# One decoder layer on one core: row numbers copied one by one for the gathered rows, and the first up loads placed behind the down loads on SyncE

## The chip, the core and the metric

The kernel runs on one core of a Trainium2 chip. The metric is device time in microseconds (us) of one execution; lower is better. Engines are named as the profile names them: PE is TensorE, DVE is VectorE, ACT is ScalarE, POOL is GpSimd, SP is SyncE, which here only issues DMAs.

## The reference, cut to what matters

One decoder layer: a mixing part (mLSTM and windowed attention), a cross-attention part, and the PEER part, in which this change lies.

```python
# per block of 128 tokens, xb: (128, 1024); 8 heads, top 16 of 128*128 experts each
qh = (xb @ w_pq)...; s1, s2 = scores against two key sets (128 keys each)
eidx, g = top 16 of the summed scores per head, softmax over them
u = expert_down[eidx]                            # rows of a 16384 x 1024 table
a = gelu(einsum('thkd,td->thk', u, xb))
out = einsum('thk,thkd->td', g * a, expert_up[eidx])
```

## The kernel before, in words

The 512 tokens are four blocks of 128. Block 0 follows the reference word for word: for each of its 128 choices per token a **fetch** (an indirect DMA on POOL, L767) brings one table row per token into one of eight buffers named `rows` (0.5 MB each), and DVE multiplies it with the tokens (L773, result in a column of `dots`); after 128 such products come 128 fetches from the up table, added up by DVE (L783, `gacc`). These 256 steps are a Python generator, `gather`; the body calls `step(ga, 1)` wherever one is to be placed.

Blocks 1 to 3 are computed densely. A **down tile** (`Down`) holds 128 experts: SP loads two tiles at a time into `draw` (L825, 1 MB, two buffers), ACT and DVE split each into a high and a low part (`dh` L790, `dl` L828), PE runs 24 matmuls (L839 to L841) into `acc_d`, and ACT applies gelu. An **up tile** (`up_tile`) needs the gates of its experts (`wt`, L873, three loads per four tiles, one for each block), the up table (`uraw`, L881, two tiles per load), and runs its matmuls at L912 to L914. There are 128 of each. Down tiles 0 to 71 are computed early, as filler beside other stages; their results go to DRAM (L863).

The gates come from two places. Those of block 1 are scattered to DRAM by POOL (L690). Those of blocks 2 and 3 are computed by `gating`: 32 steps `q` per block, in each of which DVE writes four one-hot tiles (`oh`, L744; the one for a whole step at L721 or by ACT at L725), PE multiplies them (L745, tile `w`), ACT copies the result to `stg` (L747, two buffers), and PE fills the rest of the step with nine matmuls of a down tile. Every eighth step the 2 MB in `stg` are stored to DRAM by a DMA that ACT issues (L749, `wd<-stg`).

In block 3, at the twelve odd steps from 9 to 31 (`GQ`), one step of the gather is made. After the gating come seven **lead** tiles (down tiles 72 to 78, `LEAD`), with ten gather steps among them (`GLD`), so 22 products in all before the up tiles start. The fetches of these 22 read the row numbers directly from `c.eidx`; after the lead, DVE copies the whole of `c.eidx` into `rowid` (L1209), and all later fetches read that copy and so cannot be issued before it.

The framework orders the instructions of each engine by a simulated schedule. `tc.issue_after(i)` adds an order edge for the instructions made in the block that run on the engine of `i`, and no wait. Each engine runs its list in order; so does SP with its DMA issues: one that waits for a semaphore holds all behind it.

Of the kernel before, what the change touches and what calls it, by code (L numbers as in the profile page):

```python
# [14 lines left out]
I32 = mybir.dt.int32  # L15
U32 = mybir.dt.uint32
AF = mybir.ActivationFunctionType
ALU = mybir.AluOpType
# [3 lines left out]
P = 128  # L22
# [3 lines left out]
NB = S // P  # L26
# [14 lines left out]
UG = 4  # L41
# [9 lines left out]
GQ = range(9, 32, 2)  # L51
GLD = 10
GST = 120
WST, WTL = 3, 5


LEAD = 7
# [15 lines left out]
GRP = 2  # L73
# [625 lines left out]
def gating(c, early, ga):  # L699

    nc, ps, gs, mp = c.nc, c.ps, c.gs, c.mp
    V, A, T = nc.vector, nc.scalar, nc.tensor
    for b in range(NG + NS, NB):
        tr = []
        for n_, src in (("I1T", c.I1), ("I2T", c.I2), ("gT", c.gg)):
            tp = ps.tile([P, 512], F32, tag="a", name="tp_i")
            tr_ = T.transpose(tp[:, :P], src[:, b].rearrange("p h k -> p (h k)"), c.ident)
            o = gs.tile([P, P], F32, tag=n_, bufs=1, name=n_)
            A.copy(o, tp[:, :P])
            tr.append(o)  # L710
        i1, i2, g = tr
        n1 = gs.tile([P, P], F32, tag="n1", bufs=1, name="n1")
        A.mul(n1, i1, -1.0)
        io = c.iota.unsqueeze(1).to_broadcast([P, 4, P])

        def onehot(q):

            o1 = gs.tile([P, 4, P], F32, tag="oh1", bufs=5, name="oh1")
            ib = i1[:, 4 * q:4 * q + 4].unsqueeze(2).to_broadcast([P, 4, P])
            if q % 2:  # L720
                V.tensor_tensor(o1, io, ib, op=ALU.is_equal)  # L721
            else:
                for t1 in range(4):
                    t = 4 * q + t1
                    A.activation(o1[:, t1], c.iota, AF.Abs, bias=n1[:, t:t + 1])  # L725
                A.activation(o1, o1, AF.Relu, bias=1.0, scale=-1.0)
            return o1

        oh = [onehot(q) for q in range(3)]
        if b == NG + NS:  # L730
            with c.tc.issue_after(tr_.ins):
                early.fill(FGT0)
        for q in range(32):
            if q % 8 == 0:
                stg = gs.tile([P, NK, 32], F32, tag="stg", bufs=2, name="stg")
            if q + 3 < 32:
                oh.append(onehot(q + 3))
            o1 = oh[q]
            w = ps.tile([P, 512], F32, tag="b", name="w")
            w4 = w.rearrange("p (i t) -> p i t", t=4)  # L740
            for t1 in range(4):
                t = 4 * q + t1
                o2 = gs.tile([P, P], F32, tag="oh2", bufs=4, name="oh2")
                last = V.tensor_scalar(o2, c.iota, i2[:, t:t + 1], g[:, t:t + 1], op0=ALU.is_equal, op1=ALU.mult)  # L744
                mm = T.matmul(w4[:, :, t1], o1[:, t1], o2, start=True, stop=True)  # L745
            q8 = q % 8
            A.copy(stg[:, :, 4 * q8:4 * q8 + 4], w4)  # L747
            if q8 == 7:
                nc.scalar.dma_start(c.wd[b - NG][:, :, 32 * UG * (q // 8):32 * UG * (q // 8 + 1)].rearrange("g p i -> p g i"),  # L749
                                  stg.rearrange("p (g i) t -> p g (i t)", i=UG))  # L750
            with c.tc.issue_after(mm.ins):
                early.fill(FGT)
            if b == NB - 1 and q in GQ:
                with c.tc.issue_after(c.sc[HD - 1][-1].ins), c.tc.issue_after(last.ins):
                    step(ga, 1)


def gather(c):

    nc, gp, mp = c.nc, c.gp, c.mp  # L760
    V, A, G = nc.vector, nc.scalar, nc.gpsimd
    dots = gp.tile([P, P], F32, name="dots")
    c.gacc = gp.tile([P, D], F32, name="gacc")

    def fetch(src, j):
        r = gp.tile([P, D], F32, tag="rows", bufs=8, name="rows")
        G.indirect_dma_start(out=r, out_offset=None, in_=src,  # L767
                             in_offset=bass.IndirectOffsetOnAxis(ap=c.rowid[:, j:j + 1], axis=0))
        return r

    for j in range(P):
        r = fetch(c.a["down_r"], j)
        V.tensor_tensor_reduce(r, r, c.xn0, 1.0, 0.0, op0=ALU.mult, op1=ALU.add, accum_out=dots[:, j:j + 1])  # L773
        yield
    coef = gp.tile([P, P], F32, name="coef")
    A.activation(coef, dots, AF.Gelu)
    V.tensor_tensor(coef, coef, c.gg[:, 0].rearrange("p h k -> p (h k)"), op=ALU.mult)
    for j in range(P):
        r = fetch(c.a["up"], j)
        if j == 0:  # L780
            V.tensor_scalar(c.gacc, r, coef[:, j:j + 1], None, op0=ALU.mult)
        else:
            V.scalar_tensor_tensor(c.gacc, r, coef[:, j:j + 1], c.gacc, op0=ALU.mult, op1=ALU.add)  # L783
        yield


def split3(c, pool, raw, tag, bufs):
# [29 lines left out]
class Down:  # L817


    def __init__(self, c, i2):  # L820
        nc, dp = c.nc, c.dp
        self.c, self.i2 = c, i2
        if i2 % GRP == 0:
            c.draw = dp.tile([P, GRP, D], F32, tag="draw", bufs=2, name="draw")
            nc.sync.dma_start(c.draw, c.a["down_t"][i2 // GRP])  # L825
        raw = c.draw[:, i2 % GRP]
        self.hi, self.lo = split3(c, dp, raw, "d", 2)
        c.dl = nc.vector.tensor_tensor(self.lo, raw, f32(self.hi), op=ALU.subtract)  # L828
        self.acc = None
        self.k = 0  # L830
# [36 lines left out]
def up_tile(c, u, i2, gel, acc):  # L867
    nc, up = c.nc, c.up
    V, A, T = nc.vector, nc.scalar, nc.tensor
    if i2 % UG == 0:  # L870
        c.wt = up.tile([P, ND, UG * P], F32, tag="wt", bufs=2, name="wt")
        for b in range(ND):
            i = nc.sync.dma_start(c.wt[:, b], c.wd[b][i2 // UG])  # L873
            for j in c.sc[HD - 1] if b == 0 else ():
                c.tc.add_manual_dep(i.ins, j.ins.name, SYNC, reason="gates complete")
        if i2 < SP:
            c.gsr = c.gl.tile([P, UG, TD], F32, tag="gsr", bufs=2, name="gsr")
            nc.sync.dma_start(c.gsr, c.gd[i2 // UG])
    if i2 % GRP == 0:
        c.uraw = up.tile([P, GRP, D], F32, tag="uraw", bufs=3, name="uraw")  # L880
        nc.sync.dma_start(c.uraw, c.a["up"].rearrange("(i p) d -> p i d", p=P)[:, i2:i2 + GRP])  # L881
    g = c.gsr[:, i2 % UG] if i2 < SP else gel[i2]
    raw = c.uraw[:, i2 % GRP]
    last = u == NK - 1
    if last:
        z = c.xlo.rearrange("p k t -> p (k t)")
        hi, lo = z[:, 0:D], z[:, D:2 * D]
        A.copy(hi, raw)
    else:
        hi, lo = split3(c, up, raw, "u", 2)  # L890
    V.tensor_tensor(lo, raw, f32(hi), op=ALU.subtract)  # L891
    cf = up.tile([P, TD], F32, tag="cf", bufs=2, name="cf")
    if last:
        ch, cl = z[:, 2 * D:2 * D + TD], z[:, 3 * D:3 * D + TD]
    else:
        ch = up.tile([P, TD], F32R, tag="ch", bufs=2, name="ch")
        cl = up.tile([P, TD], F32R, tag="cl", bufs=2, name="cl")
    c.cf = V.tensor_tensor(cf.rearrange("p (b t) -> p b t", t=32), g.rearrange("p (b t) -> p b t", t=32),
                    c.wt.rearrange("p b (q i t) -> p (b q) i t", q=4, i=UG)[:, :, i2 % UG], op=ALU.mult)
    A.copy(ch, cf)  # L900
    c.cl = V.tensor_tensor(cl, cf, f32(ch), op=ALU.subtract)  # L901
    return hi, lo, ch, cl
# [230 lines left out]
def body(tc, a, out, dbg=None):  # L1133
    c = Ctx()
    c.tc, c.nc, c.a = tc, tc.nc, a
    nc = c.nc
    with ExitStack() as st:
# [55 lines left out]
            ws.close()  # L1193
        c.gl = st.enter_context(pool("gels"))
        with pool("gather", side="right") as c.gp:
            c.rowid = c.eidx
            ga = gather(c)
            with pool("gating") as c.gs:
                gating(c, early, ga)
            c.up = st.enter_context(pool("up"))  # L1200
            assert len(gel) == SP

            for n in range(LEAD):
                ahead(1)
                with tc.issue_after(c.dl.ins):
                    step(ga, GLD * (n + 1) // LEAD - GLD * n // LEAD)
            c.rowid = c.gp.tile([P, P], I32, name="rowid")
            with tc.issue_after(c.dl.ins):
                nc.vector.tensor_copy(c.rowid, c.eidx)  # L1209
            pst_ = [c.ps.tile([P, 512], F32, tag=t, name="acc_u") for t in "bbbbaa"]  # L1210
            acc = [[pst_[2 * b], pst_[2 * b + 1]] for b in range(ND)]
            last, mms = [], []
            g0 = len(GQ) + GLD
            due = [WST * u + WTL * made_by(u) for u in range(-1, GST)]
            rows = [(2 * P - g0) * (d - due[0]) // (due[-1] - due[0]) for d in due]
            rows += [rows[-1]] * (NK - GST)
            for u, i2 in enumerate(up_order()):
# [49 lines left out]
def step(it, n):  # L1267
    for _ in range(n):
        next(it, None)
# [49 lines left out]
```

## Time and profile before

| | us |
|---|---|
| median of 3 runs | 1648.53 (1648.18 to 1648.61) |
| the profiled execution, its own time | 1650.35 |
| its span in the trace | 1648.70 |
| mean granted clock of TensorE | 0.991 |
| PE busy | 1605.7 (97%) |
| DVE busy | 1233.7 (75%) |
| ACT busy | 723.2 (44%) |
| POOL busy | 590.8 (36%) |

The span runs from the first to the last instruction in the trace. A stretch of the trace is named by its us from the start of the span. The last gating block runs from 781 to 866 us, the lead from there to 892, the up tiles from there to the end.

### The profile page before, as it was taken

What the parts mean: (1) busy time and instruction counts of PE and PEld (TensorE: products, weight loads), DVE (VectorE), ACT (ScalarE), POOL (GpSimd) and SP (SyncE); (2) the same over time, 40 slices, a digit from 0 to 9 for tenths busy, and PEclk for the clock granted to TensorE, in tenths of its full rate; (3) what the DMA queues carried; (4) which work ended last, traced back from release to release, by engine and by line L of the source; (5) the groups of instructions that cost most, each with busy time, mean ns of one, the idle gap of its engine ahead of it and who ended that gap; (6) DMA issues with size and microseconds to landing.
All of it is one profiled execution on the core that took longest, in us unless ns stands there. A gap on an engine that the chain in (4) does not pass through costs nothing.

```text
span 1648.7 us, 23081 instructions
## 1 busy us (share of the span) xinstructions
PE 1605.7 (97%) x8387; PEld 1411.7 (86%) x8388; DVE 1233.7 (75%) x2704; ACT 723.2 (44%) x1217; POOL 590.8 (36%) x427
## 2 busy tenths in 40 slices
PE   8998999999999999999999999999999999999994
PEld 5775698888999999999998888888888888888883
DVE  5366564564877887777787888787888888878898
ACT  5464444443544444578664333333333333333332
POOL 2000000000027787878121543443433444333451
PEclk9999999999999999999999999999999999999997
DMA  5227144232254435668999999999989999988895
GB/s 214 77 97 287 54 151 154 77 153 106 97 187 126 116 75 138 196 178 234 321 312 342 410 391 346 344 338 339 345 320 366 339 327 333 359 319 313 328 364 180
DMA packets 151122, 402.17 MB, mean 244 GB/s; under 512 B 28368, under 2 KB 62304, under 8 KB 138848
## 3 DMA queue, kind: packets, MB, share of 16 engines
q1 hardware_dynamic: 58208, 240.04, 39.4%
q0 software_dynamic: 55360, 134.32, 24.8%
q10 hardware_dynamic: 37440, 26.35, 5.1%
q8 instruction: 66, 1.08, 0.3%
q14 instruction: 48, 0.39, 0.1%
HBM read 357.07 MB, written 43.58 MB: 243 GB/s over the span
## 4 chain that ended last, share of the span: by engine, by line
PE 89%; DVE 4%; DMA 3%; ACT 1%; issue 1%; POOL 0%; DVEq 0%; SPq 0%; POOLq 0%; ACTq 0%
PE acc_u L912 10%; PE acc_u L913 10%; PE acc_u L914 10%; PE acc_d L841 10%; PE acc_d L839 10%; PE acc_d L840 10%; PE acc_f L1013 4%; PE acc_f L1015 4%; PE acc_f L1014 4%; PE w L745 3%; DMA wd<-stg 3%; PE acc_t L1026 2%; PE acc_t L1028 2%; PE acc_t L1027 2%; DVE gacc L783 1%
## 5 line engine op out<-in xcount | busy, mean ns | idle before, releaser
L839 PE MATMUL acc_d<-xhi,dh 128*128 128x384 f32 x1024 | 349.9, 342 | 1.1 <-ACT gsp L861 1.0
L841 PE MATMUL acc_d<-xhi,dl 128*128 128x384 f32 x1024 | 345.1, 337 | 1.7 <-DVE dl L828 1.7
L840 PE MATMUL acc_d<-xlo,dh 128*128 128x384 f32 x1024 | 343.7, 336 | 0.0
L913 PE MATMUL acc_u<-ul,ch 128*128 128x512 f32 x762 | 297.8, 391 | 0.0
L914 PE MATMUL acc_u<-uh,cl 128*128 128x512 f32 x762 | 296.7, 391 | 0.0
L690 POOL DMA_INDIRECT wd<-gg,ei x128 | 229.9, 1796 | 147.4 <-DVE ei L684 84.8
L912 PE MATMUL acc_u<-uh,ch 128*128 128x512 f32 x762 | 264.4, 390 | 0.1
L767 POOL DMA_INDIRECT rows<-in_up_dram,rowid x128 | 169.2, 1322 | 236.9 <-DVE gacc L783 209.0
L828 DVE TENSOR_TENSOR dl<-draw,dh 128x1024 fp32r<-128x1024 f32 x128 | 156.1, 1220 | 93.2 <-ACT dh L790 93.1
L900 ACT CAST ch<-cf 128x384 fp32r<-128x384 f32 x127 | 65.1, 514 | 356.6 <-issue 339.4
L790 ACT CAST dh<-draw 128x1024 fp32r<-128x1024 f32 x128 | 134.0, 1049 | 195.3 <-PE acc_d L840 179.4
L767 POOL DMA_INDIRECT rows<-in_down_r_dram,rowid x106 | 142.5, 1344 | 199.4 <-DVE dots L773 159.2
L839 PEld LDWEIGHTS acc_d<-xhi,dh 128*128 128x128 f32 x1024 | 192.9, 188 | 5.5 <-ACT gsp L861 1.3
L840 PEld LDWEIGHTS acc_d<-xlo,dh 128*128 128x128 f32 x1024 | 192.9, 188 | 3.7
L841 PEld LDWEIGHTS acc_d<-xhi,dl 128*128 128x128 f32 x1024 | 192.7, 188 | 4.0 <-DVE dl L828 2.6
L914 PEld LDWEIGHTS acc_u<-uh,cl 128*128 128x128 f32 x762 | 143.0, 188 | 29.4
L913 PEld LDWEIGHTS acc_u<-ul,ch 128*128 128x128 f32 x762 | 143.0, 188 | 28.7
L912 PEld LDWEIGHTS acc_u<-uh,ch 128*128 128x128 f32 x762 | 142.9, 188 | 28.3 <-ACT ch L900 0.5
L891 DVE TENSOR_TENSOR ul<-uraw,uh 128x1024 fp32r<-128x1024 f32 x127 | 154.8, 1220 | 12.4 <-ACT uh L790 11.9
L783 DVE SCALAR_TENSOR_TENSOR gacc<-rows,coef,gacc 128x1024 f32<-128x1024 f32 x127 | 162.6, 1280 | 0.9
L773 DVE CUSTOM_DVE_ANT_0 rows<-rows,xn 128x1024 f32<-128x1024 f32 x128 | 153.7, 1218 | 0.0
L901 DVE TENSOR_TENSOR cl<-cf,ch 128x384 fp32r<-128x384 f32 x127 | 70.7, 557 | 86.6 <-ACT ch L900 86.2
(344 smaller groups left out, 2644.7 us busy)
## 6 DMA issues: line engine op xcount, KB each, us to landing
draw<-in_down_t_dram SPq DMA_DIRECT2D x64, 1024.0 KB, 6.6
uraw<-in_up_dram SPq DMA_DIRECT2D x64, 1024.0 KB, 9.0
wt<-wd SPq DMA_DIRECT2D x96, 256.0 KB, 9.7
wd<-stg ACTq DMA_DIRECT2D x8, 2048.0 KB, 17.4
gd<-gsp SPq DMA_DIRECT2D x18, 768.0 KB, 3.9
gsr<-gd SPq DMA_DIRECT2D x18, 768.0 KB, 9.9
wd<-zero ACTq DMA_DIRECT2D x1, 8192.0 KB, 26.9
raw<-in_w_pq_dram SPq DMA_DIRECT2D x8, 1024.0 KB, 4.9
```

What stands on the lines that cost most here:

```text
L690: i = G.indirect_dma_start(out=out, out_offset=bass.IndirectOffsetOnAxis(ap=ei[:, h, k:k + 1], axis=0), in_=c.gg[:, NG, hh, k:k + 1], in_o ...
L767: G.indirect_dma_start(out=r, out_offset=None, in_=src, in_offset=bass.IndirectOffsetOnAxis(ap=c.rowid[:, j:j + 1], axis=0))
L773: V.tensor_tensor_reduce(r, r, c.xn0, 1.0, 0.0, op0=ALU.mult, op1=ALU.add, accum_out=dots[:, j:j + 1])
L783: V.scalar_tensor_tensor(c.gacc, r, coef[:, j:j + 1], c.gacc, op0=ALU.mult, op1=ALU.add)
L828: c.dl = nc.vector.tensor_tensor(self.lo, raw, f32(self.hi), op=ALU.subtract)
L839: T.matmul(acc[:, :TD], self.hi[:, ks], c.xhi[:, k, NG * P:], start=(k == 0), stop=False)
L840: T.matmul(acc[:, :TD], self.hi[:, ks], c.xlo[:, k, NG * P:], start=False, stop=False)
L841: T.matmul(acc[:, :TD], self.lo[:, ks], c.xhi[:, k, NG * P:], start=False, stop=(k == KT - 1))
L891: V.tensor_tensor(lo, raw, f32(hi), op=ALU.subtract)
L912: T.matmul(acc[b][n], ch[:, t], hi[:, d], start=st, stop=False)
L913: T.matmul(acc[b][n], ch[:, t], lo[:, d], start=False, stop=False)
L914: c.mm = T.matmul(acc[b][n], cl[:, t], hi[:, d], start=False, stop=sp)
```

## The change

The fetches of the first 22 rows no longer read `c.eidx`. A new tile `c.rid` has one column for each; `row_number` copies the next column of `c.eidx` into it on DVE. Sixteen of these copies are placed at the odd steps 1 to 31 of the last gating block (`GI`), each behind the one-hot tiles of its step, and six behind the splits of lead tiles 72 to 77. A fetch waits for its column. The copy of the whole `c.eidx` into `rowid` moves from behind the lead into it, behind the split of lead tile 76. The first loads of gates (`wt`) and of up tiles (`uraw`) get an order edge behind `c.lead`, the load of the last lead tiles (78 and 79). `c.row` is set and not read.

```diff
+GI = range(1, 32, 2)
...
+            if b == NB - 1 and q in GI:
+                with c.tc.issue_after(last.ins):
+                    row_number(c)
             if b == NB - 1 and q in GQ:
                 with c.tc.issue_after(c.sc[HD - 1][-1].ins), c.tc.issue_after(last.ins):
                     step(ga, 1)
...
         G.indirect_dma_start(out=r, out_offset=None, in_=src,
-                             in_offset=bass.IndirectOffsetOnAxis(ap=c.rowid[:, j:j + 1], axis=0))
+                             in_offset=bass.IndirectOffsetOnAxis(
+                                 ap=(c.rid if src is c.a["down_r"] and j < len(GQ) + GLD else c.rowid)[:, j:j + 1], axis=0))
...
+def row_number(c):
+    n = c.nid
+    if n < len(GQ) + GLD:
+        c.nc.vector.tensor_copy(c.rid[:, n:n + 1], c.eidx[:, n:n + 1])
+        c.nid += 1
...
-            nc.sync.dma_start(c.draw, c.a["down_t"][i2 // GRP])
+            c.draw_dma = nc.sync.dma_start(c.draw, c.a["down_t"][i2 // GRP])
...
         for b in range(ND):
-            i = nc.sync.dma_start(c.wt[:, b], c.wd[b][i2 // UG])
+            with c.tc.issue_after(c.lead.ins):
+                i = nc.sync.dma_start(c.wt[:, b], c.wd[b][i2 // UG])
...
-        nc.sync.dma_start(c.uraw, c.a["up"].rearrange("(i p) d -> p i d", p=P)[:, i2:i2 + GRP])
+        with c.tc.issue_after(c.lead.ins):
+            nc.sync.dma_start(c.uraw, c.a["up"].rearrange("(i p) d -> p i d", p=P)[:, i2:i2 + GRP])
...
-            c.rowid = c.eidx
+            c.rid = c.gp.tile([P, len(GQ) + GLD], I32, name="rid")
+            c.nid = 0
...
             for n in range(LEAD):
                 ahead(1)
                 with tc.issue_after(c.dl.ins):
+                    row_number(c)
+                    if n == LEAD - 3:
+                        c.rowid = c.gp.tile([P, P], I32, name="rowid")
+                        nc.vector.tensor_copy(c.rowid, c.eidx)
                     step(ga, GLD * (n + 1) // LEAD - GLD * n // LEAD)
-            c.rowid = c.gp.tile([P, P], I32, name="rowid")
-            with tc.issue_after(c.dl.ins):
-                nc.vector.tensor_copy(c.rowid, c.eidx)
+            assert c.nid == g0
+            c.lead = c.draw_dma
```

## Rows read from the trace of the kernel before

**Rows 1.** The page of the kernel before: its span, the busy time of TensorE (PE) and VectorE (DVE).

```profile
span 1648.7 us, 23081 instructions
...
PE 1605.7 (97%) x8387; PEld 1411.7 (86%) x8388; DVE 1233.7 (75%) x2704; ACT 723.2 (44%) x1217; POOL 590.8 (36%) x427
```

**Rows 2.** Busy time of each engine by stretch: the stretch in us from the start of the span, its length, the busy time of PE, PEld, DVE, ACT and POOL (instructions in brackets), the granted TensorE clock (1.00 is full speed), the busy share of the DMA engines, GB/s.

```profile
810.00:814.00 4.00, 1.89 (x13) 1.70 (x12) 2.58 (x7) 3.97 (x10) 0.00 (x0) 0.95 1.05 386
814.00:818.00 4.00, 4.00 (x20) 4.00 (x19) 2.89 (x8) 0.79 (x3) 1.15 (x1) 0.62 0.99 353
866.00:870.00 4.00, 2.75 (x15) 2.10 (x13) 1.56 (x2) 3.20 (x5) 0.00 (x0) 1.00 0.87 278
882.00:886.00 4.00, 3.22 (x17) 2.78 (x17) 3.76 (x6) 1.54 (x3) 0.00 (x0) 1.00 0.46 111
```

**Rows 3.** The chain of work that ended last, in order of time, asked for 690 to 960 us: start, us, what. A DMA in it stands with the time from issue to landing.

```profile
780.01 26.98 DMA wd<-stg
...
811.42 1.23 DVE dl L828
...
866.59 17.43 DMA wd<-stg
...
884.40 4.98 DMA uraw<-in_up_dram
...
891.92 0.50 PE acc_u L912
```

**Rows 4.** Timeline of ScalarE (ACT): the first copy into the stage buffer that waits for the store; the columns are start, us, engine, line, operation, tiles, count, and in brackets the idle time before it with its releaser.

```profile
807.06 1.08 ACT L747 COPY stg<-w 128x512 f32<-128x512 f32 x2 [4.44 <-DMA wd<-stg]
```

**Rows 5.** Timeline of TensorE in the last gating block, with the same columns.

```profile
807.79 1.05 PE L745 MATMUL w<-oh,oh 128*128 128x128 f32 x8
...
812.96 0.74 PE L745 MATMUL w<-oh,oh 128*128 128x128 f32 x4 [2.11 <-DVE oh L744]
...
819.15 1.05 PE L745 MATMUL w<-oh,oh 128*128 128x128 f32 x8
...
821.61 1.05 PE L745 MATMUL w<-oh,oh 128*128 128x128 f32 x8
```

**Rows 6.** Timeline of GpSimd (POOL): fetches of rows.

```profile
774.71 1.13 POOL L767 DMA_INDIRECT rows<-in_down_r_dram,eidx  x1 [0.30 <-issue]
...
786.38 0.94 POOL L767 DMA_INDIRECT rows<-in_down_r_dram,eidx  x1 [0.31 <-issue]
...
871.08 1.68 POOL L767 DMA_INDIRECT rows<-in_down_r_dram,eidx  x1 [6.50 <-DVE dots L773]
899.57 1.67 POOL L767 DMA_INDIRECT rows<-in_down_r_dram,rowid  x1 [26.81 <-DVE rowid L1209]
```

**Rows 7.** The line that stores the gate tile (L749), eight times in the whole run: the time from issue to landing, least, median, most.

```profile
DMA to landing us min/median/max: 12.2/17.4/27.0
```

**Rows 8.** Timeline of VectorE over one pair of gating steps that holds a row product and a down tile's split, and a wait two pairs later.

```profile
825.55 1.21 DVE L773 CUSTOM_DVE_ANT_0 rows<-rows,xn 128x1024 f32<-128x1024 f32 x1
...
830.48 1.21 DVE L773 CUSTOM_DVE_ANT_0 rows<-rows,xn 128x1024 f32<-128x1024 f32 x1
...
839.32 1.12 DVE L744 TENSOR_SCALAR oh<-iota,I2T,gT 128x128 f32<-128x128 f32 x4 [1.05 <-PE w L745]
```

**Rows 9.** Timeline of VectorE in the tail: instructions on one number a partition.

```profile
1635.04 0.15 DVE L927 TENSOR_TENSOR frst<-fss 128x1 f32<-128x1 f32 x1
1635.11 0.68 DVE L925 TENSOR_TENSOR hb<-hb,acc_u 128x512 f32<-128x512 f32 x1
```

**Rows 10.** Timeline of TensorE between the end of the gating and the first up tile.

```profile
868.85 0.45 PE L839 MATMUL acc_d<-xhi,dh 128*128 128x384 f32 x1 [1.00 <-ACT gsp L861]
...
883.52 0.44 PE L841 MATMUL acc_d<-xhi,dl 128*128 128x384 f32 x1 [0.64 <-DVE dl L828]
...
891.45 0.34 PE L841 MATMUL acc_d<-xhi,dl 128*128 128x384 f32 x1
```

**Rows 11.** Timeline of SyncE (SP) in the same stretch.

```profile
869.69 0.67 SPq L825 DMA_DIRECT2D draw<-in_down_t_dram  x1
870.67 13.69 SPq L873 DMA_DIRECT2D wt<-wd  x3
...
885.39 0.47 SPq L825 DMA_DIRECT2D draw<-in_down_t_dram  x1
```

**Rows 12.** Timeline of VectorE there.

```profile
874.75 1.23 DVE L828 TENSOR_TENSOR dl<-draw,dh 128x1024 fp32r<-128x1024 f32 x1 [0.52 <-ACT dh L790]
...
885.67 1.22 DVE L828 TENSOR_TENSOR dl<-draw,dh 128x1024 fp32r<-128x1024 f32 x1
...
890.54 2.36 DVE L891 TENSOR_TENSOR ul<-uraw,uh 128x1024 fp32r<-128x1024 f32 x2 [1.57 <-ACT uh L790]
...
895.64 1.23 DVE L828 TENSOR_TENSOR dl<-draw,dh 128x1024 fp32r<-128x1024 f32 x1 [0.87 <-ACT dh L790]
...
897.93 1.22 DVE L773 CUSTOM_DVE_ANT_0 rows<-rows,xn 128x1024 f32<-128x1024 f32 x1
```

**Rows 13.** The fetches of rows running on POOL from 861 to 863 us, and those running on POOL from 907 to 909 us: time from issue to landing.

```profile
DMA to landing us min/median/max: 4.1/4.1/4.1
...
DMA to landing us min/median/max: 13.1/13.1/13.2
```

**Rows 14.** Timeline of VectorE near the end.

```profile
1622.20 9.20 DVE L783 SCALAR_TENSOR_TENSOR gacc<-rows,coef,gacc 128x1024 f32<-128x1024 f32 x7
```

More of the change, by code (lines that the diff above doesn't have):

```diff
@@ L772, in gather @@
         r = fetch(c.a["down_r"], j)
-        V.tensor_tensor_reduce(r, r, c.xn0, 1.0, 0.0, op0=ALU.mult, op1=ALU.add, accum_out=dots[:, j:j + 1])
+        c.row = V.tensor_tensor_reduce(r, r, c.xn0, 1.0, 0.0, op0=ALU.mult, op1=ALU.add, accum_out=dots[:, j:j + 1])
         yield
@@ L782, in gather @@
         else:
-            V.scalar_tensor_tensor(c.gacc, r, coef[:, j:j + 1], c.gacc, op0=ALU.mult, op1=ALU.add)
+            c.row = V.scalar_tensor_tensor(c.gacc, r, coef[:, j:j + 1], c.gacc, op0=ALU.mult, op1=ALU.add)
         yield
+def row_number(c):
[3 more added lines that the diff above has]
+        c.nid += 1
 def split3(c, pool, raw, tag, bufs):
@@ L1201, in body @@
             assert len(gel) == SP
+            g0 = len(GQ) + GLD
             for n in range(LEAD):
@@ L1212, in body @@
             last, mms = [], []
-            g0 = len(GQ) + GLD
             due = [WST * u + WTL * made_by(u) for u in range(-1, GST)]
```

## The prediction

> **What bounds the kernel now.** I read the page first: PE is busy 97% of the span [rows 1], so the end moves only by what moves PE: its idle time, and its time at the lower clock. The windows of the stretches that the change touches show three places where PE is not full: 810 to 818, about 866 to 870, and about 882 to 886 [rows 2]. I then took the chain of waits through the first. The store of the gate tile issued at 780.01 lands 26.98 us later; ACT, which needs the buffer back, copies only at 807.06, after 4.44 us of waiting [rows 4]; its split of a down tile comes late, so DVE's low part starts at 811.42, with the one-hot tiles queued behind it [rows 3]; PE stands 2.11 us for these [rows 5]. [...] The third view is POOL's: eight fetches, 4 MB, are issued between 774.71 and 786.38 [rows 6], because only the eight free buffers held them back. The store of 27.0 us is the slowest of eight; the median is 17.4 and the fastest 12.2 [rows 7]. So the burst of fetches is the likely reason for the stall. Behind the start of the up tiles the waits show no gap of PE, and what is saved ahead of that reaches the end: the row sums that fill DVE near the end (seven in 9.2 us [rows 14]) are tied to up tiles and move with PE.
>
> **The stall at 812.** A gating step on PE takes 821.61 - 819.15 = 2.46 us; from 807.79 to 819.15 are three steps, which took 11.36 instead of 7.38 [rows 5]: 4.0 us lost, 2.1 of them idle and 1.9 at the lower clock. With the change fetch j waits for its column, copied at step 1+2j, one every 4.92 us. In the 20 us behind the store's issue fall the fetches of steps 1, 3, 5 and 7, instead of the end of a burst of eight. I expect the store near the median, landing near 798, and ACT needs its buffer only after its first copy of the next eight steps, about 802.6 (807.06 less the 4.44 [rows 4]). About 2 us more could pass before PE is hit, since ACT's 4.4 cost PE 2.1. So all 4.0 us go. Next late there is DVE, below. The bounds are 0 (the store stays late) and -4.0; I take **-4.0**, because even the median store leaves 4 us of margin.
>
> **The copies.** No row shows a copy of one column; the nearest are instructions on one number a partition: 0.15 us long, with the next one starting 0.07 us after [rows 9]. DVE is full in the last gating block: a pair of steps with a row product and a down split takes 830.48 - 825.55 = 4.93 us [rows 8], against 4.92 for two steps on PE. A pair without a split leaves DVE waiting 1.05 us for PE [rows 8], which hides a copy. Two steps use 18 of the 24 matmuls of a down tile, so three pairs of four hold a split: from step 9 on 9 of 12 pairs. The cost is 9 x 0.07 = 0.6 to 9 x 0.15 = 1.4 us; below nothing it can't go, since a copy takes no work away. I take **+0.6**, for a copy starts behind other DVE work as that row does. The copies of steps 1 to 7 lie where there is no product yet, the six in the lead where DVE waits for ACT; those are nothing, unless DVE becomes the last there (first rival).
> [...]
>
> **Fetches and products.** In the gating a fetch is issued eight steps, 19.7 us, ahead of its product; a fetch lands in 4.1 us when the DMA engines are quiet and in 13.2 in a burst [rows 13]. So nothing waits there. In the lead the distance shrinks: rows 20 and 21 are copied behind the splits of tiles 76 and 77, and their products stand behind that of tile 78. Before, the last of the 22 was issued at 871.08 and the next at 899.57 [rows 6]. I take **0** and price the rest as a rival.
>
> **The loads on SP.** SP issues the load of tiles 76/77 at 869.69, then stands at the `wt` loads, 13.69 us for the three, because the third waits for the last gate store; the load of 78/79 follows only at 885.39 [rows 11]. Its buffer is free when tile 75 has been split, at 874.75 + 1.1 = 875.9 [rows 12]: 9.5 us late. PE did not stand for that, since the order gave it up tiles first: it runs its last down matmul at 891.45 and its first up matmul at 891.92 [rows 3, 10], 0.3 more than a matmul's step. With the change the load goes out near 876 and the `wt` and `uraw` loads queue behind it; they could not have been used earlier anyway, for the store issued at 866.59 lands after 17.43 [rows 3]. PE can then run tile 78 first: 45 matmul steps lie between 883.52 and 891.45 [rows 10], 0.176 us each, so a tile of 24 is 4.2 us of cover for the chain store, `wt`, `uraw`, split. Gain at most 0.3; loss up to what the first rival says. The copy of all row numbers only moves. I take **0**: 0.3 back, and as much for 1 MB of rows and 1 MB of draw added ahead of the store's landing.
>
> **Sum.** -4.0 + 0.6 + 0 = -3.4 us against the profiled execution's own 1650.35 (1.65 above its span): 1646.95. The median of the runs is 1648.53, 1.8 lower; it gives **1645.1**.
>
> **Rivals.** (1) **The lead gives it back, and more.** Row 21 is copied after the split of tile 77, 885.67 + 1.1 = 886.8 [rows 12]. With 0.4 to its issue and a landing of 13.2 it is there at 900.4; if DVE's order has its product ahead of the first up tile's parts, these wait till 901.6 and PE gets them at about 903.2, 1.6 later (1.2 split, 0.4 cast). PE is through with tile 78 at 891.6 + 4.2 = 895.8: 7.4 us idle, and 1.9 at the lower clock as at 814. -3.4 + 9.3 = +5.9: 1654.4. It decides from a landing of about 8 us. For it: the last products had 8 rows of lead before, now one tile, and rows 22 and on follow in a burst. Against: the order of DVE may well put the up parts first, as it had them ahead of the split of 78 (890.54 against 895.64 [rows 12]). Chance 0.18.
> The same place is reached if the last store takes 27.0 us, as in the burst, instead of 17.4, because fetches and draw now run through it: first up matmul at 901.5, 5.7 idle, +1.9: 1652.7. [...]
> (2) **More is gained.** The idle of the lead, 4.00 - 2.75 and 4.00 - 3.22 [rows 2], 2.0 us, comes from late splits [rows 10]; an order in which tile 72 does not overtake the last gating step would free it: 1643.1. For it: both gaps follow from one late split; against: nothing in the change addresses that. Chance 0.22.
> (3) **Half is given back**: copies at 0.15 us (+0.8) and the draw and rows in the lead late by 1 us: 1646.9. Chance 0.16.
> (4) **It doesn't do what it says**: the store is late from other loads, and only the copies count: 1648.53 + 0.6 = 1649.1. Against: the 27.0 is the only such one, beside the only burst. Chance 0.06.
>
> **Numbers.** My forecast has 0.38. A measurement of this kernel tells about 0.2% (3.3 us) from no change. The forecast lies at -3.4, so of its 0.38 I count 0.27 as faster and 0.11 as the same. Faster: 0.27 + 0.22 = 0.49; same: 0.11 + 0.16 + 0.06 = 0.33; slower: 0.18. The range takes in rival 2 with the whole 0.3 and no cost of copies (1643.1 - 0.3 - 0.6 = 1642.2, taken down to 1641.5 because PE's first matmuls behind a gap are slow too) and the milder half of rival 1 (up to 1652.5).
>
> **What would show it.** POOL's fetches 4.9 us apart from 783 on; the store of 780 landing under 20 us; no idle of PE and clock 1.00 between 806 and 822; a pair of steps on DVE at 5.0 us; the load of 78/79 near 876 less 4, PE running tile 78 before the first up matmul. I am wrong if PE or DVE stands for a row in the lead, if the last store takes over 20 us, or if copies hold DVE for more than 0.15 us each, say by a wait for POOL.

## The result, and the profile after

The changed kernel takes **1657.09 us** (median of 4 runs, 1655.25 to 1660.13) against 1648.53: a ratio of 1.0052, 95% interval 1.0039 to 1.0064. It is slower by 0.5%, above the predicted range. The profiled execution took 1655.25 us, the fastest of the four, and that of before 1650.35, so the two traces hold 4.9 of the 8.6 us between the medians.

I cut both traces at two events that they share: the issue of the last gate store (the end of the gating) and the start of the last matmul. **A** runs from the store issued at 780 us to the last gate store, **B** from there to the last matmul, **C** from there to the end of the span.

| | A | B | C | span |
|---|---|---|---|---|
| before | 86.6 | 760.3 | 21.9 | 1648.7 |
| after | 83.1 | 764.7 | 26.5 | 1653.5 |
| after less before | -3.5 | +4.4 | +4.6 | +4.8 |

(The store at 780 was issued 0.8 us earlier in the trace of after, ahead of all that the change touches; that makes up the sum.)

**A went as predicted.** Timeline of GpSimd after the change (start, us, what, and in brackets the idle time before it with its releaser):

```profile
782.45 1.71 POOL L773 DMA_INDIRECT rows<-in_down_r_dram,rid  x1 [8.89 <-ACT oh L729]
787.23 0.96 POOL L773 DMA_INDIRECT rows<-in_down_r_dram,rid  x1 [3.07 <-PE acc_d L856]
...
878.51 1.81 POOL L773 DMA_INDIRECT rows<-in_down_r_dram,rid  x1 [4.82 <-DVE rowid L1228]
...
885.63 0.93 POOL L773 DMA_INDIRECT rows<-in_down_r_dram,rowid  x1 [0.30 <-issue]
...
890.59 0.94 POOL L773 DMA_INDIRECT rows<-in_down_r_dram,rowid  x1 [0.30 <-issue]
```

The burst of eight [rows 6] has become one fetch every 4.9 us from 782 on. In this trace nothing waits for the store of 780, so it has no landing; in three kernels below with the same copies it lands after 17.5, 17.6 and 17.5 us (copies_only, gating_copies, early_rid) instead of 27.0. The store's line in copies_only, asked for 776 to 784 us:

```profile
DMA to landing us min/median/max: 17.5/17.5/17.5
```

Busy time by stretch, with the columns of [rows 2]:

```profile
810.00:814.00 4.00, 4.00 (x29) 4.00 (x29) 3.92 (x13) 2.01 (x5) 1.68 (x1) 1.00 1.09 397
814.00:818.00 4.00, 4.00 (x31) 4.00 (x30) 3.12 (x9) 3.17 (x8) 1.67 (x1) 1.00 1.03 420
890.00:894.00 4.00, 0.94 (x6) 0.62 (x4) 1.48 (x3) 0.89 (x3) 1.22 (x2) 1.00 0.93 341
894.00:898.00 4.00, 3.88 (x12) 3.56 (x13) 2.09 (x4) 1.05 (x3) 0.00 (x0) 0.59 1.03 420
```

PE is full between 810 and 818 and the clock is 1.00. But the lower two rows show a new hole: 0.94 of 4 us busy, and then a clock of 0.59. In the timeline of VectorE a copy of one column takes 0.14 us, and the next instruction starts 0.06 after it, close to the two values that the prediction weighed (0.15 and 0.07):

```profile
857.87 0.14 DVE L798 COPY rid<-eidx 128x1 int32<-128x1 int32 x1
857.93 1.21 DVE L780 CUSTOM_DVE_ANT_0 rows<-rows,xn 128x1024 f32<-128x1024 f32 x1
```

**B: the hole at 890.** B as a whole, before and after, with the columns of [rows 2]:

```profile
866.59:1626.85 760.26, 758.10 (x3632) 663.54 (x3630) 627.27 (x796) 267.76 (x369) 313.37 (x235) 1.00 0.92 343
862.28:1627.02 764.74, 760.26 (x3632) 665.17 (x3630) 622.99 (x797) 267.76 (x369) 320.07 (x238) 1.00 0.92 341
```

PE stands 4.5 us where it stood 2.2, and the same 3632 matmuls keep it busy 2.2 us longer. Both come from one place. The chain of work that ended last, in order of time (start, us, what):

```profile
862.28 24.29 DMA wd<-stg
...
886.59 5.81 DMA wt<-wd
```

The last gate store took 24.29 us, where it took 17.43 [rows 3]. The first gates (`wt`) follow it. Then ScalarE and TensorE:

```profile
893.11 0.51 ACT L917 CAST ch<-cf 128x384 fp32r<-128x384 f32 x1 [5.42 <-DVE cf L915]
893.53 0.48 ACT L872 ACTIVATE gel<-acc_d 128x384 f32<-128x384 f32 x1
```

```profile
894.07 0.44 PE L854 MATMUL acc_d<-xhi,dh 128*128 128x384 f32 x1 [3.13 <-ACT gel L872]
894.35 0.34 PE L855 MATMUL acc_d<-xlo,dh 128*128 128x384 f32 x1
894.74 0.69 PE L856 MATMUL acc_d<-xhi,dl 128*128 128x384 f32 x1
895.22 0.52 PE L854 MATMUL acc_d<-xhi,dh 128*128 128x384 f32 x1
895.54 0.52 PE L855 MATMUL acc_d<-xlo,dh 128*128 128x384 f32 x1
```

This is a wait that passes through the order of three engines. PE stands 3.13 us for `gel` of a down tile, whose matmuls were long done; `gel` stands on ACT behind `ch`, which waits 5.42 us for `cf` on VectorE, which waits 6.86 us for `wt`. PE did run a lead tile first, as predicted, but the next down tile needs the PSUM that `gel` frees. Then matmuls follow each other every 0.32 us instead of 0.17 until 898.1, at the lower clock.

Why the store is late, by the DMA queues while it is in flight (862.3 to 886.6 us; packets, MB, share of 16 engines' time; q10 is the gate store, q0 the row fetches, q1 SP's loads):

```profile
q1 hardware_dynamic: 720, 3.41, 36.2%
q0 software_dynamic: 886, 3.19, 35.4%
q10 hardware_dynamic: 4112, 2.10, 28.8%
```

In the flight of before's last store q1 moved 2.36 MB and q0 0.75.

SP's loads moved too (start, us from the first issue to the last of the group):

```profile
865.40 6.65 SPq L840 DMA_DIRECT2D draw<-in_down_t_dram  x2
872.40 14.51 SPq L889 DMA_DIRECT2D wt<-wd  x3
```

**C: the end.** Timeline of VectorE:

```profile
1622.37 13.17 DVE L790 SCALAR_TENSOR_TENSOR gacc<-rows,coef,gacc 128x1024 f32<-128x1024 f32 x10
1635.73 1.28 DVE L790 SCALAR_TENSOR_TENSOR gacc<-rows,coef,gacc 128x1024 f32<-128x1024 f32 x1 [0.20 <-DMA rows<-in_up_dram,rowid]
1637.05 1.29 DVE L942 TENSOR_TENSOR hb<-hb,gacc 128x512 f32<-128x512 f32 x2
```

Eleven row sums are left when the last up tile has been split, where seven were [rows 14]: four times 1.3 us. Of the 256 products and sums, 243 stand in VectorE's list ahead of the last up tile's last split, and 247 did before; the list is three or four behind from about the twentieth up tile on, and never makes it up.

### The profile page after: what moved, and what is told of

Its sections match the earlier page's. It is cut to its first block, busy times and chain, and to the rows that moved or that the text cites. A ratio compares the mean times of both kernels' runs of the same rounds, so it can differ in the third digit from the quotient of the medians.

```text
span 1653.5 us, 23108 instructions
## 1 busy us (share of the span) xinstructions
PE 1606.7 (97%) x8387; PEld 1411.6 (85%) x8388; DVE 1235.8 (75%) x2726; ACT 723.5 (44%) x1217; POOL 601.9 (36%) x427
## 3 DMA queue, kind: packets, MB, share of 16 engines
q0 software_dynamic: 55360, 134.32, 24.8%
## 4 chain that ended last, share of the span: by engine, by line
PE 64%; issue 18%; POOL 11%; DVE 4%; DMA 2%; ACT 1%; POOLq 0%; DVEq 0%; another core or an unknown queue 0%; ACTq 0%
POOL rows L773 10%; PE acc_d L856 7%; PE acc_d L854 7%; PE acc_d L855 7%; PE acc_u L930 4%; PE acc_u L931 4%; PE acc_u L929 4%; PE acc_f L1030 4%; PE acc_f L1031 4%; PE acc_f L1032 4%; PE w L748 3%; PE acc_t L1043 2%; PE acc_t L1044 2%; PE acc_t L1045 2%; DMA wd<-stg 1%
## 5 line engine op out<-in xcount | busy, mean ns | idle before, releaser
L929 PE MATMUL acc_u<-uh,ch 128*128 128x512 f32 x762 | 260.4, 390 | 0.0
L805 ACT CAST uh<-uraw 128x1024 fp32r<-128x1024 f32 x127 | 133.1, 1049 | 3.0 <-DMA uraw<-in_up_dram 3.0
```

Of the source, the lines that this page charges most:

```text
L805: c.nc.scalar.copy(hi, raw)
L929: T.matmul(acc[b][n], ch[:, t], hi[:, d], start=st, stop=False)
```

## The experiments

All of them together, with the same cuts; "fetches" are the row fetches issued in the 30 us behind the issue of the last gate store, and "last sums" the row sums in VectorE's list behind the last up tile. Medians and ratios are against runs of the kernel before on the same chip.

| | median us | ratio (95%) | A | B | C | last store us | fetches | last sums |
|---|---|---|---|---|---|---|---|---|
| before | 1648.53 | 1 | 86.6 | 760.3 | 21.9 | 17.4 | 1 | 7 |
| after | 1657.09 | 1.0052 (1.0039 to 1.0064) | 83.1 | 764.7 | 26.5 | 24.3 | 11 | 11 |
| order_only | 1649.25 | 1.0000 (0.9989 to 1.0010) | 86.6 | 759.7 | 21.8 | 19.9 | 3 | 7 |
| copies_only | 1658.53 | 1.0061 (1.0044 to 1.0078) | 83.2 | 766.5 | 26.3 | 20.7 | 10 | 11 |
| gating_copies | 1652.63 | 1.0022 (1.0012 to 1.0032) | 83.1 | 768.7 | 19.6 | 24.8 | 4, and 2 just ahead | 6 |
| early_rid | 1659.05 | 1.0062 (1.0045 to 1.0079) | 83.1 | 775.5 | 19.6 | 32.8 | 10 | 6 |
| after_spread | 1652.36 | 1.0014 (1.0005 to 1.0024) | 83.3 | 765.1 | 22.2 | 20.5 | 8 | 7 |
| late_rowid | 1660.37 | 1.0076 (1.0059 to 1.0093) | 83.1 | 770.4 | 26.6 | 23.8 | 10 | 11 |
| spread | 1648.02 | 0.9989 (0.9980 to 0.9998) | 83.2 | 760.9 | 21.8 | 18.0 | 1 | 7 |

The store at 780 itself is issued between 779.1 (after_spread) and 780.8 us (copies_only). These 1.7 us arise ahead of all that the change touches, so a difference of medians of that size says little by itself; the argument goes by A, B and C.

**order_only**: the kernel before, with the order edges on SP alone.

```diff
+            with c.tc.issue_after(c.lead.ins):
+                i = nc.sync.dma_start(c.wt[:, b], c.wd[b][i2 // UG])
...
+        with c.tc.issue_after(c.lead.ins):
+            nc.sync.dma_start(c.uraw, ...)
```

> The kernel before with the order edges alone, no copies. Theory A: the stall at 812 us stays (27 us for the store issued at 780), the row sums are not behind, so 1646 to 1650 us. Theory B: 1651 us or more, with TensorE idle at the first up tiles.

Nothing changes: the store of 780 and the stall (chain, and timeline of PE) stay as in [rows 3, 5].

```profile
780.17 27.02 DMA wd<-stg
```

```profile
813.17 1.05 PE L745 MATMUL w<-oh,oh 128*128 128x128 f32 x4 [2.16 <-DVE oh L744]
```

On SP the loads of the last lead tiles now go ahead of the gates (start, us to the last of the group):

```profile
869.87 6.67 SPq L825 DMA_DIRECT2D draw<-in_down_t_dram  x2
876.89 10.09 SPq L874 DMA_DIRECT2D wt<-wd  x3
```

The third `wt` load waits for the last store, which was issued at 866.77; the group ends at 886.98. In before it ended 0.34 us behind the store's landing, so here the store takes about 19.9 us instead of 17.4. B is not longer for that: the seventh tile, now ahead of the up tiles on PE, covers it. The loads behind the seven down tiles cost nothing and bring nothing by themselves; how much cover is left was not measured.

**copies_only**: the changed kernel without those edges.

```diff
-            with c.tc.issue_after(c.lead.ins):
-                i = nc.sync.dma_start(c.wt[:, b], c.wd[b][i2 // UG])
+            i = nc.sync.dma_start(c.wt[:, b], c.wd[b][i2 // UG])
...
-        with c.tc.issue_after(c.lead.ins):
-            nc.sync.dma_start(c.uraw, ...)
+        nc.sync.dma_start(c.uraw, ...)
```

> The changed kernel without the order edges behind the last lead load: only the copies and the earlier copy of all row numbers. Theory A (the copies in the lead do the harm: they put fetches and so traffic beside the last gate store, and they leave VectorE's order of row sums four behind to the end): between 1652 and 1662 us, with the last gate store over 20 us and ten or more row sums in a row at the end. Theory B (the order edges do the harm, since the gate and up loads then queue behind the load of tiles 78/79): 1644 to 1647 us, the gain of the gating stage alone.

As slow as the whole change, with both losses. Here the loss in B shows at the up tiles: the store lands after 20.68 us, and the up load behind it takes 7.57 instead of 4.98 [rows 3]; PE stands 5.12 us for its split.

```profile
863.99 20.68 DMA wd<-stg
885.05 7.57 DMA uraw<-in_up_dram
```

So both losses come with the copies, the early copy of all row numbers among them. Before, order_only, copies_only and after make a square: the last store takes 17.4, 19.9, 20.7 and 24.3 us, and B is 760.3, 759.7, 766.5 and 764.7. The edges and the copies each make the store later, and only the copies make B longer.

**gating_copies**: sixteen copies in the gating as in the change, but the last takes rows 15 to 21 at once; the copy of all row numbers behind the lead, no edges.

```diff
-        c.nc.vector.tensor_copy(c.rid[:, n:n + 1], c.eidx[:, n:n + 1])
-        c.nid += 1
+        m = 1 if n < len(GI) - 1 else len(GQ) + GLD - n
+        c.nc.vector.tensor_copy(c.rid[:, n:n + m], c.eidx[:, n:n + m])
+        c.nid += m
...
```

> The kernel before with the sixteen copies in the gating alone; the last of them copies the columns of rows 15 to 21 at once, so the fetches of the lead are held back only by their buffers, as before; the copy of all row numbers stands behind the lead, and there are no order edges. Theory A: the 4.0 us of the stall less 0.7 for the copies, and one row sum fewer at the end (1.3): 1643 to 1646 us, the last gate store near 17 us, seven row sums or fewer in a row at the end. Theory B gives the same. If the paced fetches themselves cost something later, 1648 us or more.

That expectation failed: I had taken the copies in the lead for the cause. Without them C is short (six sums left), yet B is worse. With only 16 of 20 rows fetched at the end of the gating, the free buffers let a new burst out, six fetches from 861.71 to 868.25, which the store issued at 863.76 meets at its start; it takes 24.84 us, and PE, after standing 4.27 us for `gel` as in the changed kernel, is at half clock at 894:

```profile
894.00:898.00 4.00, 3.70 (x9) 2.69 (x10) 4.00 (x8) 3.46 (x5) 0.00 (x0) 0.50 1.03 406
```

One thing more differs from before here: SP's order came out as with the edges, though there are none. Both `draw` loads are issued from 866.87 on and the `wt` loads only from 873.86; in order_only that alone made the store 2.4 us later.

**early_rid**: the changed kernel, with the six columns of the lead copied at the last gating step.

```diff
+        m = 1 if n < len(GI) - 1 else len(GQ) + GLD - n
+        c.nc.vector.tensor_copy(c.rid[:, n:n + m], c.eidx[:, n:n + m])
...
-            assert c.nid == g0
```

> The changed kernel with the lead's six columns copied at the last gating step; the copy of all row numbers stays inside the lead and the order edges stay. Theory A: the row sums are one ahead of before in VectorE's order and not four behind, so the tail is short; rows 22 and on are still fetched beside the last store and the first up loads, so part of the stall at the first up tile may stay: 1643 to 1650 us. Theory B: 1650 us or more, since the edges are there.

Both bursts now meet the store: the one at its start and the one that the copy of all row numbers lets out within the lead. The store is in flight 32.77 us (chain), and PE stands 10.63 us for `gel`, as in the changed kernel:

```profile
862.34 32.77 DMA wd<-stg
```

```profile
900.82 0.69 PE L855 MATMUL acc_d<-xhi,dh 128*128 128x384 f32 x1 [10.63 <-ACT gel L873]
```

With these two a new theory stood: the burst was not removed but postponed. Copying at step 1+2j leaves four buffers empty at the end of the gating (16 rows fetched, 12 multiplied), and whatever then delivers row numbers fills them at once, into loads that have less slack than the store of 780 had. The square below tests it: sixteen or twenty rows in the gating, all row numbers within the lead or behind it.

**spread**: gating_copies with four more copies.

```diff
-GI = range(1, 32, 2)
+GI = sorted([*range(1, 32, 2), 10, 16, 22, 28])
```

> The change's copies in the gating, but twenty instead of sixteen: one at each odd step and one more at steps 10, 16, 22 and 28, the last of them taking rows 19 to 21 at once; row numbers for rows 22 and on behind the lead and SyncE's order as before. So the buffers are as full at the end of the gating as in the kernel before. My theory (the change moves fetches off the store of 780 onto the last store of the gates, which has less slack): the stall at 812 stays gone, the last store lands in about 17 us with one or two fetches in its flight, wt and uraw follow as before, no half clock behind 890, the tail has 7 row sums: 1645, 1643 to 1647. The rival (copies one by one cost what they gain wherever the fetches lie, by VectorE's and GpSimd's waits): 1651 or more, with a last store of 17 us.

The stall is gone and nothing else is late. Chain; GpSimd; the queues while the store is in flight (863.6 to 881.6); VectorE near the end:

```profile
863.59 18.00 DMA wd<-stg
...
881.97 5.07 DMA uraw<-in_up_dram
```

```profile
868.08 1.68 POOL L773 DMA_INDIRECT rows<-in_down_r_dram,rid  x1 [5.60 <-DVE dots L780]
897.20 1.68 POOL L773 DMA_INDIRECT rows<-in_down_r_dram,rowid  x1 [27.44 <-DVE rowid L1227]
```

```profile
q10 hardware_dynamic: 4112, 2.10, 38.7%
...
q0 software_dynamic: 329, 1.15, 19.5%
```

```profile
1619.85 9.21 DVE L790 SCALAR_TENSOR_TENSOR gacc<-rows,coef,gacc 128x1024 f32<-128x1024 f32 x7
```

A is 83.2, B 760.9, C 21.8: A's gain is kept, and the span is 2.4 us shorter than before's. The medians differ by 1.7 us (before has 1649.68 on that chip), 0.11% (0.02 to 0.20%): less than the 1645 expected, but the only version faster than both kernels. SP's order is that of before here, so spread differs from gating_copies in 1 MB of `draw` ahead of the gates as well as in the four copies.

**after_spread**: the change itself with the same four copies more; the diff is that of spread.

> The changed kernel with the same twenty copies in the gating; rows 20 and 21 copied in the lead, the copy of all row numbers after the lead's fifth tile and the order on SyncE stay as changed. VectorE's order then has no row sum deferred (247 of 256 before the last up tile's last split, as before; the changed kernel 243). My theory: two losses add up in the changed kernel, the last store (about 5 us) and four row sums at the end (about 4.7 us). Here the second is gone and the first is less (three to six fetches in the store's flight, landing in 18 to 22 us): 1647, 1645 to 1651. The rival (one loss alone, the late store, which the tail only passes on): the tail stays at ten or more row sums wherever the store is late.

```profile
862.39 20.45 DMA wd<-stg
882.85 5.04 DMA wt<-wd
888.15 24.26 DMA draw<-in_down_t_dram
```

```profile
890.00:894.00 4.00, 3.77 (x13) 3.77 (x14) 3.41 (x7) 0.74 (x1) 2.10 (x2) 0.59 1.02 420
```

```profile
1622.81 9.21 DVE L790 SCALAR_TENSOR_TENSOR gacc<-rows,coef,gacc 128x1024 f32<-128x1024 f32 x7
```

C is back to seven sums: 4.3 us shorter than after's, with B as long as after's. So C does not depend on the late store, and the rival of that expectation falls. What I had wrong is that B would lose less: the store landed 3.8 us sooner than after's, and B stayed at 765.1. VectorE and TensorE show where it was lost:

```profile
888.01 1.03 DVE L915 TENSOR_TENSOR cf<-gel,wt 128x384 f32<-128x384 f32 x2 [3.65 <-DMA wt<-wd]
```

```profile
890.23 0.45 PE L856 MATMUL acc_d<-xhi,dl 128*128 128x384 f32 x1 [1.92 <-DVE dl L843]
```

PE stands for the low part `dl` of a down tile, which stands on VectorE behind `cf`, which waits for `wt` behind the store; then comes the lower clock, 0.59. So it is again the last store, late with only three fetches in its flight but with the edges' 1 MB of `draw`. The load of the next down tiles, issued at 888.15 in the midst of the fetches, took 24.26 us, where the one issued at 885.39 before [rows 11] took 9.1. It is on the chain that ended last, but PE stood only 0.72 us behind it, at 922.11. How much B would lose by that load alone, and whether the fetches alone make it slow, was not tried; in spread, which has not the loss, the burst of `rowid` fetches starts only at 897.20.

**late_rowid**: the change with the copy of all row numbers behind the lead.

```diff
-                    if n == LEAD - 3:
-                        c.rowid = c.gp.tile([P, P], I32, name="rowid")
-                        nc.vector.tensor_copy(c.rowid, c.eidx)
                     step(ga, GLD * (n + 1) // LEAD - GLD * n // LEAD)
-            assert c.nid == g0
+            c.rowid = c.gp.tile([P, P], I32, name="rowid")
+            with tc.issue_after(c.dl.ins):
+                nc.vector.tensor_copy(c.rowid, c.eidx)
```

> The changed kernel with one line moved: the copy of all row numbers stands behind the lead, as before the change; sixteen copies in the gating and six in the lead, the order on SyncE as changed. With the changed kernel, after_spread and spread this makes a square of two sizes: sixteen or twenty rows copied in the gating, and all row numbers within the lead or behind it. My theory (two losses that add up): the store has five fetches in flight where the changed kernel has seven, lands in 19 to 21 us, and PE ends one to three us earlier; VectorE's order still has four row sums deferred (243 of 256), so the tail has ten or eleven row sums: 1652, 1650 to 1655. The rival (the tail is only long because the store is late): tail of seven row sums, 1648 or less.

The tail came as expected (ten sums and one more), the rest did not: 1660.37, 8 us above my value. GpSimd, ScalarE, TensorE and VectorE:

```profile
886.51 0.97 POOL L773 DMA_INDIRECT rows<-in_down_r_dram,rowid  x1 [0.30 <-issue]
...
893.14 1.30 POOL L773 DMA_INDIRECT rows<-in_down_r_dram,rowid  x1 [0.30 <-issue]
```

```profile
913.47 1.04 ACT L805 CAST dh<-draw 128x1024 fp32r<-128x1024 f32 x1 [11.01 <-DMA draw<-in_down_t_dram]
```

```profile
914.57 0.44 PE L854 MATMUL acc_d<-xhi,dh 128*128 128x384 f32 x1 [2.86 <-ACT dh L805]
```

```profile
1628.06 13.17 DVE L790 SCALAR_TENSOR_TENSOR gacc<-rows,coef,gacc 128x1024 f32<-128x1024 f32 x10
```

The burst of `rowid` fetches, six from 886.51 to 893.14, now goes out into the loads of the up stage: the load of two down tiles issued at 890.09 lands after 23.36 us, and PE stands for it until 914.57. Besides these 2.86 us PE stands another 5.1 us within B, where before has 2.2 in all, and it runs at the lower clock behind the waits: 0.62 from 914 to 918, 0.52 from 918 to 922. The store itself still took 23.75 us with five fetches in its flight, against 24.29 with seven: the two `rowid` fetches that met it in after were worth about 0.5 us of it. A burst moved behind the store is not gone either; here it hits the next load. It need not cost anything: before sends out eight fetches from 899.57 on [rows 6], spread eight from 897.20 on, and in neither does PE wait in the 30 us from there.

The square: with twenty rows, moving the copy of all row numbers behind the lead takes B from 765.1 to 760.9; with sixteen it takes B from 764.7 to 770.4. Spread is not a clean corner: it has no edges, and no row number is copied singly in the lead. From sixteen to twenty rows C falls from 26.5 to 22.2 and from 26.6 to 21.8.

## Why the prediction was wrong

**The stall and the copies: right.** -4.0 + 0.6 = -3.4 was the sum for the gating; A measures -3.5, and -3.3 to -3.5 in all seven kernels with copies. Of the 4.0, 1.9 were laid to the lower clock behind the idle time: before, the granted clock was 0.62 from 814 to 818 [rows 2]; after, it was 1.00. The cause, a burst of fetches through the store, holds too: order_only keeps the burst and the stall, all others lose both.

**"Fetches and products ... 0" and "The loads on SP ... 0": the steps that failed.** I counted 1 MB of rows and 1 MB of draw added ahead of the last store's landing and gave them 0.3 us, set off against 0.3 of gain. The draw alone is worth 2.4 us of the store's time, and hidden (order_only); the fetches alone are worth 3.3 (copies_only); both together 6.9 (after). The trace shows 3.19 MB of rows in its flight where 0.75 were, and 11 fetches in 30 us where one was. I had seen that fetch j waits for its column, but I had not counted how many buffers that leaves empty: 16 fetched less 12 multiplied is four ahead, not eight. Five of the seven fetches issued in the store's flight read `rid`: they are the paced ones themselves, come late. With the copy of all row numbers moved into the lead, nothing holds the rest back. I wrote that this copy "only moves"; it releases the fetches of rows 22 and on, which stood until 899.57 before [rows 6]. That it costs anything by itself is not shown. Moved back, with all else as changed, B is 5.6 us longer and not shorter (late_rowid). Spread has 4.2 us less in B than after_spread, but there two late copies and the edges differ too.

**The first rival, second route, came true in the main.** It had the last store at 27.0 and PE 5.7 us idle plus 1.9 at the lower clock, 1652.7. Measured: 24.29 us, 3.13 idle, and nine matmul steps of about 0.32 instead of 0.17 us. I gave the first rival a chance of 0.18, although the same sort of burst stood in the trace with its price. A last store of over 20 us was among its own signs of being wrong. In its 24.29 us of flight the store's queue had 28.8% of the 16 engines' time, SP's loads 36.2 and the fetches 35.4%; before, where the fetches had 11.8% and SP's loads 38.4, it had 40.6%. The first route, a late product of row 21, did not come: VectorE stood only 0.72 us for a row in the lead.

**"Tied to up tiles and move with PE": wrong.** In no case of the prediction did the end get longer than PE's. It is half the loss in the trace: four row sums of 1.3 us. They are placed by VectorE's order, and what counts is where the last row numbers of the 22 are copied. With six single copies in the lead eleven sums are left (after, copies_only, late_rowid); with the same six columns copied at the last gating step six are left (gating_copies, early_rid); with two in the lead, seven (after_spread). Twenty copies instead of sixteen remove just this, with all else of the change in place. Why the order doesn't catch up over more than a hundred up tiles was not tried.

**Left open.** The profiled execution of after is its fastest; the 1.8 us to its median have no trace. B's loss is in no simple proportion to the fetches: six around the start of the store cost gating_copies 8.4 us, ten later ones cost copies_only 6.2, and gating_copies has 1 MB of draw ahead of the gates besides. Their place against the loads may count, and so may the different orders on ACT; neither was tried by itself. And spread gains 1.7 us by its medians, 2.4 by its span.

## What to carry to other kernels

Whoever paces a burst of prefetches has to follow the buffers to the end of the paced stretch: if fewer are full there than before (here four ahead instead of eight), the burst is not removed but postponed, and its new place is to be priced by the transfer that it meets and that one's slack (here the last store, 24.3 us instead of 17.4). A copy that a gather waits for is a gate; to move it is to move all that it lets out (late_rowid: six fetches beside a load that then took 23.36 us). Work that is dealt out in an engine's fixed order did not move with the bottleneck here (eleven row sums left instead of seven): count what is left of it at the end, before and after.

## What the runs showed of the hardware that I had not expected

The time of the same 2 MB gate store goes by what the other queues move in its flight (row fetches and SP's loads together):

| | MB of others | store, us |
|---|---|---|
| before | 3.1 | 17.4 |
| spread | 3.5 | 18.0 |
| order_only | 4.3 | 19.9 |
| after_spread | 4.6 | 20.5 |
| copies_only | 4.9 | 20.7 |
| late_rowid | 6.1 | 23.8 |
| after | 6.6 | 24.3 |
| gating_copies | 6.7 | 24.8 |
| early_rid | 9.8 | 32.8 |

That is about 2 us for each MB more, for rows (copies_only) as for draw (order_only); a longer flight also takes in more, so what one MB by itself costs is not shown. A load of two down tiles took 9.1 us before (the one of 885.39), and others took 23 to 24 when a burst of fetches went out beside it (after_spread, late_rowid), with SP's own loads in flight too. The engine that issues a fetch spends 0.9 to 2.8 us on it; the price was paid by another queue's transfer.
